# A decoder block on one core: the beginning of the attention in another order, the row sums a step later, and the gated branch's output products in halves

## The chip, the core and the metric

The kernel runs on one core of one Trainium2 chip. The time is the device time of one execution in microseconds (us); the figure for a kernel is the median of its runs. The profile is that of one execution, taken by the hardware profiler; its times count from the start of its span. PE is TensorE, DVE is VectorE, ACT is ScalarE, POOL is GpSimd and SP is SyncE, whose queue issues nearly all DMAs.

## The reference, cut to what matters

The block takes 1024 tokens of width 1024 in float32. From one projection of the normalised input come the queries, keys and values of eight heads of width 64, their forget gates, and the two inputs of a gated branch of width 512. The results of both are put side by side and go through one output matrix:

```python
c = jnp.cumsum(log_f, axis=1)
logits = einsum('bqhd,bkhd->bhqk', qi, k) * scale + ci[..., None] - c_k
p = softmax(where(causal, logits, -inf))
att = einsum('bhqk,bkhd->bqhd', p, v)
mixed = einsum('gij,bnjgd->bnigd', tril(w_s), rmsnorm(vg)) + b_s     # in chunks of 128 tokens
sg = u * mixed
h = x + concatenate([att, sg]) @ w_out
h = h + conv_ffn(rmsnorm(h))                                        # gated, causal convolution of width 3
out = rmsnorm(h)
```

So `att` meets rows 0 to 511 of `w_out` and `sg` rows 512 to 1023; the two partial products can be made at different times and added.

## The kernel before

Every float32 operand of a product is split in two parts, high and low (`[:, 0]` and `[:, 1]` of a tile), and a product is three matmuls: high by high, high by low, low by high. The splits are made by ACT (a copy, the cast) and DVE (a subtraction). The kernel has these parts in order of time: projections of the input (to about 214 us in the profile); the spatial products of the gated branch; the attention, head after head (to 387); the product of the attention's output with `w_out`; the second norm; the feed-forward part, 22 column blocks and then the down projection.

**Order.** A scheduling pass puts the instructions of each engine in an order, by the program's order and by when it reckons their operands to be ready, and each engine then runs its own in that order. `after(tc, later, earlier)` (line 60) forces an order of two instructions of one engine. `seq` (673) does so for every PE instruction of the attention, so that PE runs those in exactly the program's order. The class `Line` (30) wraps ACT, DVE and POOL: while it is `on`, each call stands behind the one before; while it is off and its `last` is set, each call stands behind that one instruction.

**Banks.** PSUM has eight banks, held by pools: `psa` for the projections and the spatial products (tags `b` and `s`, four banks each), `psb` from line 762 on for the attention (tag `b`, four banks, and tag `L`, two tiles of two banks for the logits), `psc` for what follows. A pool gives its banks to tags in the order in which the tags are first used. A tile of the next pool waits for what used its bank in the pool before.

**End of the projections** (710 to 720). The last products of the values fill four `s` banks. `spatial` (679) computes `mixed`: for each of eight groups three matmuls into a `b` bank and two DVE operations that add the bias and multiply by `u` in place in `ut`. `evac_v` (655) empties a bank of values into `V`, with ACT for the high part and DVE for the low. A small exponential (719) is there to have ACT's table of that function loaded.

**Beginning of the attention** (912 to 920). `head_loads(h)` (766) issues five DMAs for a head: queries `qd`, keys `kd` three times (512 KB, 256 KB, 256 KB), and a broadcast of the summed gates `ncd` (512 KB); the queries are 512 KB too, so a head is 2 MB. `turn_sg(hf)` (698) transposes half of the gated branch's result: four banks with four 128x128 transposes each, and the two parts of the split from each bank. `logits(h, j)` (778) takes query block j of head h: matmuls over the keys 0 to (j+1)*128 into an `L` tile, a mask on POOL (790), a DVE operation that adds the gates and keeps the least value `mn` (798), and ACT's exponential, which also adds up the row (800). The mask of block j changes columns that the DVE operation of block j+1 reads, so it waits for that one. Head 0's eight blocks come first of all, from j = 7 down.

**Attention steps** (921 to 943). A head has five steps. In each, `turn_p` (802) transposes two pairs of key blocks of the probabilities for the next step (a bank each, copied by ACT and subtracted by DVE into `pt`, 814 and 815); `values` (818) multiplies the present ones with `V` into the bank `po`, which ACT and DVE empty twice a head (840, 841); and one or two blocks of the next head's logits follow each. At step 1 `row_tail` (733) inverts the head's eight row sums (738), transposes them (739), sends them to memory and loads them back in another layout (741, 742); `pair_half` (745) multiplies by them, for heads 0 to 5 on POOL, for the last pair on DVE (756 to 758).

**Fillers.** `sg_out` (845) is a generator with the gated branch's products with `w_out`. It loads the weights of one half of the columns (`wos`, two DMAs of 512 KB), splits them (`split`, ACT and POOL), and then makes 16 products, each of 128 tokens by 512 columns: twelve matmuls over four blocks of the contraction into one bank, an addition of `x` on DVE (877), a store to `hpd` (878). `fill(key)` (908) takes the next product, as often as the table `FILLS` (21) says for that place: once after j = 5, 3 and 0 of head 0's logits (key (-1, j)), and in heads 0 to 4 after steps 0, 2, 4 (even heads) or 1, 3 (odd heads). Heads 5 to 7 have none.

**After the attention.** `wmm` (1022) makes the product with the other rows of `w_out`, of which the loop at 1086 does three quarters of the contraction for eight banks before the last heads' part is needed.

Of the kernel before, what the change touches and what calls it, by code (L numbers as in the profile page):

```python
# [65 lines left out]
def block_kernel(ctx: ExitStack, tc: tile.TileContext, xT, xtok, wuv, wv, wqk, wf, cpk, bfv,  # L66
# [37 lines left out]
    def f32(ap):  # L104
        return ap.bitcast(F32)
# [549 lines left out]
    def evac_v(tt, ps):  # L655
        if tt % 2 == 0:
            V.append(sb("V", [P, 2, 8, 2, 64], F32R))
        v = V[tt // 2]
        p3 = ps.rearrange("p (h d) -> p h d", h=8)
        act.activation(v[:, tt % 2, :, 0, :], p3, AF.Copy, scale=rstd1[:, tt:tt + 1])  # L660
        dve.scalar_tensor_tensor(out=v[:, tt % 2, :, 1, :], in0=p3, scalar=rstd1[:, tt:tt + 1],
                                 in1=f32(v[:, tt % 2, :, 0, :]), op0=ALU.mult, op1=ALU.subtract)

    for p_ in range(2):
        t = ring(F32)
# [32 lines left out]
    def turn_sg(hf):  # L698

        for c in range(4):  # L700
            if hf == 0:
                sgT[c] = sb("G", [P, 2, 1024], F32R)
            ps = bank()
            for t in range(4):
                seq(pe.transpose(ps[:, t * P:(t + 1) * P], ut[hf][:, t, c * P:(c + 1) * P], ident))
            o = slice(hf * 512, hf * 512 + 512)
            act.copy(sgT[c][:, 0, o], ps)
            dve.tensor_tensor(out=sgT[c][:, 1, o], in0=ps, in1=f32(sgT[c][:, 0, o]), op=ALU.subtract)

    S = [sbank() for _ in range(4)]  # L710
    for k in range(4):
        tmul(S, w0[k], "T3", k, True)
        pool.tensor_tensor(out=wvr[k][:, 1, :], in0=wvr[k][:, 0, :], in1=wvr[k][:, 1, :], op=ALU.add)
    tprod(S, lambda k: wvr[k][:, 1, :], "B22", False)
    spatial()
    for m in range(4):
        evac_v(4 + m, S[m])

    act.activation(pad[:, 0:1], eps, AF.Exp)
    act.last = dve.last = None  # L720


# [53 lines left out]
        rows[h] = sml.tile([P, 8], F32, tag="rs", name=nm("rs"))  # L776

    def logits(h, j):


        i, jj, hh = j // 2, j % 2, h % 2
        A, B, ck, B2 = abs_[h][:, 0, :], abs_[h][:, 1, :], cks[:, hh, :], b2s[:, hh, :]
# [10 lines left out]
        ps = psa.tile([P, 1024], F32, tag="L", bufs=2, name=nm("pl"))  # L793
        for c in range(0, n, 512):
            e = min(n, c + 512)
            seq(pe.matmul(ps[:, c:e], A[:, qs], B[:, c:e], start=True, stop=False))  # L796
            seq(pe.matmul(ps[:, c:e], A[:, qs], B2[:, c:e], start=False, stop=True))  # L797
        dve.tensor_tensor_reduce(out=t, in0=ps[:, 0:n], in1=ck[:, 0:n], scale=1.0, scalar=lim[:, 0:1],  # L798
                                 op0=ALU.add, op1=ALU.min, accum_out=mn)
        exs.append(act.activation(t, t, AF.Exp, bias=mn, scale=-1.0, accum_out=rows[h][:, j:j + 1]))  # L800

    def turn_p(g):
# [42 lines left out]
    def sg_out():  # L845
# [14 lines left out]
            return whs  # L860

        whs = split(load(0), "pool")
        for hf in range(2):
            o = slice(hf * 512, hf * 512 + 512)
            for tt in range(8):
                if hf == 0 and tt == 6:
                    nxt = load(1)
                ts_ = slice(tt * P, (tt + 1) * P)
                hs = sb("raw", [P, 512])
                sp.dma_start(out=hs, in_=xtok[ts_, o])  # L870
                ps = fbank()
                for k in range(4):
                    w = whs[k]
                    seq(pe.matmul(ps, sgT[k][:, 0, ts_], w[:, 0, :], start=(k == 0), stop=False))  # L874
                    seq(pe.matmul(ps, sgT[k][:, 0, ts_], w[:, 1, :], start=False, stop=False))  # L875
                    seq(pe.matmul(ps, sgT[k][:, 1, ts_], w[:, 0, :], start=False, stop=(k == 3)))  # L876
                dve.tensor_tensor(out=hs, in0=ps, in1=hs, op=ALU.add)
# [32 lines left out]
            next(filler, None)  # L910

    head_loads(0)
    head_loads(1)
    turn_sg(0)
    for j in range(7, -1, -1):
        logits(0, j)
        if j == 6:
            turn_sg(1)
        fill((-1, j))
    turned = [turn_p(g) for g in STEPS[0]]  # L920
    for n, step in enumerate(STEPS):
# [3 lines left out]
        if h == 7 and s == 0:  # L925
# [590 lines left out]
```

## Time and profile before

| | us |
|---|---|
| median of 3 runs | 1076.2 (1076.04 to 1078.09) |
| the profiled execution | 1076.44 |
| its span | 1074.7 |
| PE busy | 1054.8 (98%) |
| PE weight loads busy (beside PE) | 875.8 (81%) |
| DVE busy | 892.9 (83%) |
| ACT busy | 571.0 (53%) |
| POOL busy | 237.2 (22%) |

How to read its rows. In a timeline a row has start, duration, engine, line of the code, operation, output tile <- input tiles, shape, and how many instructions were put together; in brackets stands how long the engine was idle before, and what it waited for. A row of the view of waits has waiter <- what it waited for: total us, times, longest. A row of the chain of waits has start, duration and what that stretch was spent on. Where `Line` makes the call the line is that of the helper, L44, and tiles tell the operations apart. A matmul's row is longer (0.39 us for 512 columns) than its distance to the next one in a row of matmuls, since they overlap.

### The profile page before, as it was taken

How to read it: one execution, taken by the hardware profiler on the slowest of the kernel's cores; microseconds unless marked ns; L12 is line 12 of the kernel's file. 1: busy time of each engine (PE TensorE's matmuls, PEld its weight loads, DVE VectorE, ACT ScalarE, POOL GpSimd, SP SyncE). 2: the span in 40 equal slices, each digit the busy share in tenths (PEclk: the TensorE clock that was granted, in tenths of full speed). 3: DMA queues.
4: the chain of work that ended last, by engine and by line, in shares of the span. 5: the costliest groups of instructions: out<-in, count | busy, mean ns of one | idle time of the engine just before them, and what ended most of it. 6: DMA issues, size and time to landing. Idle time of an engine off the chain costs nothing.

```text
span 1074.7 us, 14461 instructions
## 1 busy us (share of the span) xinstructions
PE 1054.8 (98%) x5013; PEld 875.8 (81%) x5013; DVE 892.9 (83%) x1303; ACT 571.0 (53%) x985; POOL 237.2 (22%) x219
## 2 busy tenths in 40 slices
PE   9999999989999899999999999999999999999997
PEld 6888788778888788878888888888888888888886
DVE  5985798777777869999899999989988776898774
ACT  6666644456666845764444444444444444454653
POOL 0002134020223651054333333333322000000000
PEclk9999999999999999999999999999999999999999
DMA  9242257957556335132244523223331899433442
GB/s 338 97 140 97 68 159 213 265 165 215 162 177 225 120 128 185 72 118 97 98 137 161 172 69 127 99 98 99 107 118 46 289 327 319 123 95 97 140 125 96
DMA packets 66297, 160.80 MB, mean 150 GB/s; under 512 B 7976, under 2 KB 8240, under 8 KB 66224
## 3 DMA queue, kind: packets, MB, share of 16 engines
q1 hardware_dynamic: 65792, 159.32, 45.5%
q8 instruction: 39, 0.64, 0.2%
q10 hardware_dynamic: 432, 0.57, 0.1%
q14 instruction: 34, 0.28, 0.1%
HBM read 117.06 MB, written 42.80 MB: 149 GB/s over the span
## 4 chain that ended last, share of the span: by engine, by line
PE 74%; DVE 2%; issue 2%; DMA 2%; ACT 2%; POOL 0%; DVEq 0%; ACTq 0%; POOLq 0%; SPq 0%
PE k L1369 19%; PE qa L1117 11%; PE qc L1117 11%; PE qd L1117 11%; PE qb L1117 5%; PE pb L832 2%; PE pb L813 2%; PE pf L874 1%; PE pf L876 1%; PE pf L875 1%; PE pl L796 1%; PE pl L797 1%; DMA raw<-wos 1%; PE pb L1026 1%; PE pb L1028 1%
## 5 line engine op out<-in xcount | busy, mean ns | idle before, releaser
L1369 PE MATMUL k<-whb,wha 128*128 128x512 f32 x924 | 209.7, 389 | 0.0
L1369 PEld LDWEIGHTS k<-whb,wha 128*128 128x128 f32 x924 | 173.3, 188 | 36.2 <-DVE wha L160 0.2
L1117 PE MATMUL qc<-xT,whb 128*128 128x512 f32 x540 | 129.8, 389 | 0.0
L1117 PE MATMUL qa<-xB,wha 128*128 128x512 f32 x528 | 127.2, 390 | 0.0
L1117 PEld LDWEIGHTS qc<-xT,whb 128*128 128x128 f32 x540 | 101.3, 188 | 21.2 <-ACT whb L154 0.2
L1117 PEld LDWEIGHTS qa<-xB,wha 128*128 128x128 f32 x528 | 98.8, 188 | 20.8 <-DVE wha L160 0.4
L154 ACT CAST wha<-sg 128x512 fp32r<-128x512 f32 x77 | 47.7, 622 | 96.9 <-PE k L1369 86.6
L154 ACT CAST whb<-sg 128x512 fp32r<-128x512 f32 x82 | 50.6, 618 | 85.8 <-PE qc L1117 68.5
L160 DVE TENSOR_TENSOR wha<-sg,wha 128x512 fp32r<-128x512 f32 x77 | 52.8, 688 | 41.0 <-ACT wha L154 40.9
L1117 PE MATMUL qd<-xB,whb 128*128 128x512 f32 x264 | 63.8, 389 | 0.5 <-DVE h L1236 0.5
L1117 PE MATMUL qd<-xT,whb 128*128 128x512 f32 x264 | 63.6, 389 | 0.0
L815 DVE TENSOR_TENSOR pt<-pb,pt 128x512 fp32r<-128x512 f32 (+1 forms) x80 | 50.0, 635 | 14.5 <-ACT pt L814 13.4
L160 DVE TENSOR_TENSOR whb<-sg,whb 128x512 fp32r<-128x512 f32 x82 | 58.3, 711 | 4.4 <-ACT whb L154 4.3
L1117 PE MATMUL qb<-xT,whb 128*128 128x512 f32 x252 | 60.8, 389 | 0.0
L1004 POOL TENSOR_TENSOR sg<-raw 128x512 f32<-128x512 f32 x20 | 30.9, 1546 | 134.2 <-DVE whb L160 76.0
L1117 PEld LDWEIGHTS qd<-xB,whb 128*128 128x128 f32 x264 | 49.5, 188 | 11.2 <-issue 0.9
L1117 PEld LDWEIGHTS qd<-xT,whb 128*128 128x128 f32 x264 | 49.5, 188 | 10.3
L1117 PEld LDWEIGHTS qb<-xT,whb 128*128 128x128 f32 x252 | 47.3, 188 | 9.8
L814 ACT CAST pt<-pb 128x512 fp32r<-128x512 f32 (+1 forms) x80 | 42.5, 539 | 20.6 <-PE pb L813 14.7
L832 PE MATMUL pb<-pt,V 128*128 128x256 f32 x320 | 51.4, 285 | 1.3 <-DVE pt L815 1.2
L790 POOL TENSOR_SCALAR_AFFINE_SELECT x<-x 128x128 f32<-128x128 f32 x64 | 19.9, 312 | 129.7 <-DVE mn L798 77.4
L1007 POOL TENSOR_TENSOR sg<-sg,raw 128x512 f32<-128x512 f32 x20 | 33.3, 1664 | 64.1 <-DVE whb L160 64.1
(396 smaller groups left out, 2305.7 us busy)
## 6 DMA issues: line engine op xcount, KB each, us to landing
raw<-wup SPq DMA_DIRECT2D x44, 512.0 KB, 3.7
sg<-hx SPq DMA_DIRECT2D x77, 256.0 KB, 2.6
hx<-hs SPq DMA_DIRECT2D x44, 256.0 KB, 3.8
hx<-ca SPq DMA_DIRECT2D x35, 256.0 KB, 2.0
xT<-wdn SPq DMA_DIRECT2D x28, 256.0 KB, 4.3
raw<-wqk SPq DMA_DIRECT2D x8, 512.0 KB, 3.6
qd<-G SPq DMA_DIRECT2D x16, 256.0 KB, 3.5
kd<-G SPq DMA_DIRECT2D x16, 256.0 KB, 3.3
```

The source lines that it names most:

```text
L154: act.copy(h, src)
L160: return eng.tensor_tensor(out=l, in0=src, in1=f32(h), op=ALU.subtract)
L790: sels[h].append(pool.affine_select(out=ck[:, qs], in_=ck[:, qs], pattern=[[-1, P]], compare_op=ALU.is_ge, fill=BIG, base=0, channel_multi ...
L796: seq(pe.matmul(ps[:, c:e], A[:, qs], B[:, c:e], start=True, stop=False))
L813: seq(pe.transpose(ptr[:, c:c + P], tj[jj][:, k * P:(k + 1) * P], ident))
L814: act.copy(pt[:, 0, 0:w], ptr[:, 0:w])
L815: dve.tensor_tensor(out=pt[:, 1, 0:w], in0=ptr[:, 0:w], in1=f32(pt[:, 0, 0:w]), op=ALU.subtract)
L832: seq(pe.matmul(po[0][:, oo:oo + n], lhs, pt[:, s, o:o + n], start=(k == 0 and s == 0), stop=(s == 1 and half)))
L1004: pool.tensor_tensor(out=s[0], in0=a21, in1=a22, op=ALU.add)
L1007: pool.tensor_tensor(out=s[3], in0=s[1], in1=a12, op=ALU.add)
L1117: pe.matmul(ps, w[:, wi, ks], xb[:, xi, k, :], start=(first and n == 0), stop=(n == 11), skip_group_check=True)
L1369: pe.matmul(banks[bk + m], xh[:, xi, ms], wh[:, wi, :], start=(first and p_ == 0 and n == 0), stop=(p_ == NP - 1 and n == 2), skip_group_c ...
```

## The change

Six edits, which belong together:

1. The four evictions of values come before `spatial` in the program, and the small exponential is ordered behind the last of them on ACT.
2. `sg_out` stops once after its first load and split, and this first part runs right after `head_loads(0)`, ahead of `head_loads(1)`; its ACT instructions are ordered behind the last eviction of values.
3. `logits` is cut in two, `logits_mm` (the matmuls) and `logits_end` (mask, minimum, exponential). Head 0's matmuls for j = 7 and 6 come ahead of `turn_sg(0)`, their ends behind its last DVE operation; then comes `turn_sg(1)`, then the fillers and the other blocks.
4. A filler is cut in two halves of the contraction, each with a bank, six matmuls and a DVE addition of its own; the store follows the second. The split of the second weights goes in two parts behind the halves of the eighth product.
5. `FILLS` counts halves: two after j = 6, 4 and 2 and one after j = 0 of head 0, and one in each of the 25 steps of heads 0 to 4. That makes 32 halves for the 16 products.
6. `row_tail` comes at step 2 of a head in place of step 1.

```diff
-FILLS = {(-1, j): 1 for j in (5, 3, 0)} | {(h, s): 1 for h in range(5) for s in ((0, 2, 4), (1, 3))[h % 2]}
+FILLS = {(-1, 6): 2, (-1, 4): 2, (-1, 2): 2, (-1, 0): 1} | {(h, s): 1 for h in range(5) for s in range(5)}
...
     tprod(S, lambda k: wvr[k][:, 1, :], "B22", False)
+    for m in range(4):
+        a = evac_v(4 + m, S[m])
+
+    after(tc, act.activation(pad[:, 0:1], eps, AF.Exp), a)
     spatial()
-    for m in range(4):
-        evac_v(4 + m, S[m])
-
-    act.activation(pad[:, 0:1], eps, AF.Exp)
     act.last = dve.last = None
...
+    def logits_mm(h, j):
+        A, B, B2 = abs_[h][:, 0, :], abs_[h][:, 1, :], b2s[:, h % 2, :]
+        n = (j + 1) * P
+        qs = slice(j * P, (j + 1) * P)
+        ps = psa.tile([P, 1024], F32, tag="L", bufs=2, name=nm("pl"))
+        for c in range(0, n, 512):
+            e = min(n, c + 512)
+            seq(pe.matmul(ps[:, c:e], A[:, qs], B[:, c:e], start=True, stop=False))
+            seq(pe.matmul(ps[:, c:e], A[:, qs], B2[:, c:e], start=False, stop=True))
+        return ps
+
+    def logits_end(h, j, ps, behind_=None):
...
+        if behind_ is not None:
+            after(tc, m, behind_)
...
         whs = split(load(0), "pool")
+        yield
...
-                ps = fbank()
-                for k in range(4):
-                    w = whs[k]
-                    seq(pe.matmul(ps, sgT[k][:, 0, ts_], w[:, 0, :], start=(k == 0), stop=False))
-                    seq(pe.matmul(ps, sgT[k][:, 0, ts_], w[:, 1, :], start=False, stop=False))
-                    seq(pe.matmul(ps, sgT[k][:, 1, ts_], w[:, 0, :], start=False, stop=(k == 3)))
-                dve.tensor_tensor(out=hs, in0=ps, in1=hs, op=ALU.add)
-                sp.dma_start(out=hpd[tt, :, o], in_=hs)
-                if hf == 0 and tt == 7:
-                    whs = split(nxt, "dve")
-                yield
+                for kh in range(2):
+                    ps = fbank()
+                    for k in (2 * kh, 2 * kh + 1):
+                        w = whs[k]
+                        seq(pe.matmul(ps, sgT[k][:, 0, ts_], w[:, 0, :], start=(k % 2 == 0), stop=False))
+                        seq(pe.matmul(ps, sgT[k][:, 0, ts_], w[:, 1, :], start=False, stop=False))
+                        seq(pe.matmul(ps, sgT[k][:, 1, ts_], w[:, 0, :], start=False, stop=(k % 2 == 1)))
+                    dve.tensor_tensor(out=hs, in0=ps, in1=hs, op=ALU.add)
+                    if kh == 1:
+                        sp.dma_start(out=hpd[tt, :, o], in_=hs)
+                    if hf == 0 and tt == 7:
+                        whs[2 * kh:2 * kh + 2] = split(nxt[2 * kh:2 * kh + 2], "dve")
+                    yield
...
     head_loads(0)
+    act.last = a
+    next(filler)
+    act.last = None
     head_loads(1)
-    turn_sg(0)
-    for j in range(7, -1, -1):
+    ahead_ = [(j, logits_mm(0, j)) for j in (7, 6)]
+    d = turn_sg(0)
+    for j, ps in ahead_:
+        logits_end(0, j, ps, d)
+    turn_sg(1)
+    fill((-1, 6))
+    for j in range(5, -1, -1):
         logits(0, j)
-        if j == 6:
-            turn_sg(1)
         fill((-1, j))
...
-        if s == 1:
+        if s == 2:
             if h % 2 == 0:
                 attF[h // 2] = sb("H", [P, 2, 1024])
             row_tail(h)
```

More of the change, by code (lines that the diff above doesn't have):

```diff
@@ L659, in evac_v @@
         p3 = ps.rearrange("p (h d) -> p h d", h=8)
[L660 removed]
+        a = act.activation(v[:, tt % 2, :, 0, :], p3, AF.Copy, scale=rstd1[:, tt:tt + 1])
         dve.scalar_tensor_tensor(out=v[:, tt % 2, :, 1, :], in0=p3, scalar=rstd1[:, tt:tt + 1],
                                  in1=f32(v[:, tt % 2, :, 0, :]), op0=ALU.mult, op1=ALU.subtract)
+        return a
     for p_ in range(2):
@@ L707, in turn_sg @@
             act.copy(sgT[c][:, 0, o], ps)
-            dve.tensor_tensor(out=sgT[c][:, 1, o], in0=ps, in1=f32(sgT[c][:, 0, o]), op=ALU.subtract)
+            d = dve.tensor_tensor(out=sgT[c][:, 1, o], in0=ps, in1=f32(sgT[c][:, 0, o]), op=ALU.subtract)
+        return d
     S = [sbank() for _ in range(4)]
@@ L778, in logits @@
     def logits(h, j):
+        logits_end(h, j, logits_mm(h, j))
+    def logits_mm(h, j):
[9 more added lines that the diff above has]
+    def logits_end(h, j, ps, behind_=None):
         i, jj, hh = j // 2, j % 2, h % 2
-        A, B, ck, B2 = abs_[h][:, 0, :], abs_[h][:, 1, :], cks[:, hh, :], b2s[:, hh, :]
+        ck = cks[:, hh, :]
         w1, w2 = (2 * i + 1) * P, (2 * i + 2) * P
@@ L792, in logits @@
         mn = sml.tile([P, 1], F32, tag="mn", name=nm("mn"))
[L793 to L799, printed above, removed]
+        m = dve.tensor_tensor_reduce(out=t, in0=ps[:, 0:n], in1=ck[:, 0:n], scale=1.0, scalar=lim[:, 0:1],
+                                     op0=ALU.add, op1=ALU.min, accum_out=mn)
+        if behind_ is not None:
+            after(tc, m, behind_)
         exs.append(act.activation(t, t, AF.Exp, bias=mn, scale=-1.0, accum_out=rows[h][:, j:j + 1]))
```

## The prediction

> **What bounds the kernel now.** I read the page first, then the busy times of three windows, then what TensorE (PE) waited for, then the timelines of PE, VectorE (DVE) and ScalarE (ACT) at those waits. "Step" below is one of the five attention steps of a head.
>
> ```profile
> span 1074.7 us, 14461 instructions
> PE 1054.8 (98%) x5013; PEld 875.8 (81%) x5013; DVE 892.9 (83%) x1303; ACT 571.0 (53%) x985; POOL 237.2 (22%) x219
> ```
>
> PE is busy for 98% of the span, so the change can win only where PE waits. It touches three stretches: from the end of the spatial products to the first transposes of probabilities; heads 0 to 4, which have fillers; heads 5 to 7, which have none. The windows view gives one row for each (its length, then the busy us and instructions of PE, weight loads, DVE, ACT and POOL, the granted clock, and the DMA's share and GB/s):
>
> ```profile
> 219.60:239.55 19.95, 16.84 (x93) 14.07 (x92) 15.11 (x33) 14.28 (x29) 7.06 (x11) 1.00 0.36 128
> 239.55:346.40 106.85, 104.77 (x670) 91.99 (x669) 80.42 (x164) 69.51 (x151) 25.04 (x53) 1.00 0.64 195
> 346.40:387.10 40.70, 35.66 (x274) 32.83 (x272) 33.21 (x69) 31.96 (x70) 24.36 (x36) 1.00 0.37 121
> ```
>
> PE is idle for 3.11, 2.08 and 5.04 us: 10.2 us is all that could be won if every gap in the three closed. DVE is the next busiest: 80.42 of 106.85 us where the fillers are. The view of waits says whom PE waited for between 219 and 400 us (us in total, times, longest):
>
> ```profile
> PE pb L813 <- DVE pt L815: 2.9, 6, 0.7
> PE pb L739 <- DVE rs L738: 2.6, 2, 1.5
> PE pb L705 <- DVE V L44: 1.9, 1, 1.9
> PE pb L832 <- DVE pt L815: 1.2, 3, 0.6
> PE pl L796 <- DVE mn L798: 1.2, 2, 0.7
> ```
>
> Every wait is for DVE: for a bank that it has yet to empty (L813, L705, L796), or for its result. L739 is the row sums' transposition; the change moves it.
>
> **Part 1, the beginning of the attention.** Its rows, DVE, ACT and PE:
>
> ```profile
> 213.06 2.11 DVE L44 SCALAR_TENSOR_TENSOR V<-ps,rstd,V 128x512 fp32r<-128x512 f32 x3 [2.84 <-ACT V L44]
> 215.09 6.35 DVE L44 SCALAR_TENSOR_TENSOR A<-pb,cp,A 128x256 f32<-128x256 f32 x16
> 221.35 0.74 DVE L44 SCALAR_TENSOR_TENSOR V<-ps,rstd,V 128x512 fp32r<-128x512 f32 x1
> 223.86 2.48 DVE L708 TENSOR_TENSOR G<-pb,G 128x512 fp32r<-128x512 f32 x4 [1.77 <-ACT G L707]
> 212.33 2.73 ACT L44 ACTIVATE V<-ps,rstd 128x512 fp32r<-128x512 f32 x4 [4.81 <-PE ps L258]
> 220.94 2.40 ACT L154 CAST whl<-raw 128x512 fp32r<-128x512 f32 x4 [5.88 <-DMA raw<-wos]
> 226.98 1.28 ACT L800 ACT_TABLE_LOAD   x1
> 222.15 1.53 PE L705 MATMUL pb<-ident,A 128*128 128x128 f32 x12 [1.93 <-DVE V L44]
> 225.25 1.91 PE L705 MATMUL pb<-ident,A 128*128 128x128 f32 x16
> 239.55 1.80 PE L813 MATMUL pb<-ident,t 128*128 128x128 f32 x15
> ```
>
> Before, one V eviction stood behind the sixteen gating operations, and the transposes of the gated branch waited for its bank until 222.15. With the four V evictions first, DVE does them from 213.06 to 215.8 (4 x 0.70) and the gating to 222.15 (+6.35). DVE's work is only reordered: it ends as late as before. What is won is what PE does meanwhile: the logits of j = 7 and 6 (1.8 us before: from the end of the twelve transposes, 0.11 us each after 222.15, to 225.25) go into the 1.93 us gap, if head 0's operands are there; by the chain they had landed at 210.42:
>
> ```profile
> 203.47 6.95 DMA x<-kd
> 210.50 11.69 DMA raw<-wos
> ```
>
> A pool gives its banks out in the order of first use: before, the transposes came first and got the banks of V (hence their wait for V). Now the logits come first and get those, and the transposes get the banks of the spatial products, the last of which DVE frees at 222.15. If the first transposes fall on that one, PE waits for 0.9 us at 221.3; if on the first freed one, not at all. I take the wait, since before the second transposes fell on the bank emptied last.
>
> From 222.15 on: 16 transposes take 1.9 us (to 224.1); DVE subtracts at 0.6 us each and ends the first half at about 225.7 (226.34 before). It then has the minima of j = 7 and 6 (1.27 and 1.14 us), and only then the second half's subtractions, except one that fits where the minimum of j = 6 waits for its mask. All four banks are held by the second half, so the first half filler starts at about 227.6 and the second at 229.25: PE idles for 1.7 us here, a new wait. After that PE has six half fillers and the logits of j = 5 to 0. A whole filler is twelve matmuls:
>
> ```profile
> 232.27 0.39 PE L874 MATMUL pf<-whl,G 128*128 128x512 f32 x1
> 234.99 0.33 PE L796 MATMUL pl<-x 128*128 128x384 f32 x1
> ```
>
> From its first matmul to what follows it 2.72 us pass, so a half is 1.36. Six halves are 8.2 us and the logits 2.5, which makes 240.0; with the kind bank order 239.0. I take 239.6, against 239.55: **0.0 us**, between -0.9 and +0.8, with 3.5 fillers done in place of 3. Three things hang on covers. The weights' load (1 MB) is issued ahead of head 1's five loads. By the second of those rows it took 11.69 us before with head 1's 2 MB and 0.25 MB of head 0 ahead of it, 0.28 MB per us; behind head 0 alone it lands about 4.6 us after 210.4, at 215, so its four casts (2.40 us) stand on ACT before 222, where the copies of the transposes begin; if it landed at 222 as before, the copies and all behind them would be 1.7 us later. Head 1's loads come 3.6 us later; they landed before 222, and their logits begin only after the transposes at 239.55. The exponential's table load (1.28 us) goes to 215, where ACT is idle; before it delayed no exponential that PE waited for. What the new loads queue behind on SP is head 0's, which have to land first anyway.
>
> **Part 2, half a filler in each step.** Heads 0 to 4 hold 25 halves for 13 whole fillers: **-1.36 us** of PE, which part 1 has taken over. Of the 2.08 us that PE is idle in these heads, five waits for `pt` make 1.67 (a first one of 0.20 for its values, four of transposes for a bank, of 0.26 to 0.7; the first and the last of these):
>
> ```profile
> 258.24 0.63 PE L813 MATMUL pb<-ident,H 128*128 128x128 f32 x4 [0.26 <-DVE pt L815]
> ...
> 341.91 0.63 PE L813 MATMUL pb<-ident,H 128*128 128x128 f32 x4 [0.26 <-DVE pt L815]
> ```
>
> The four stand at the end of a head, where transposes follow a step that had no filler: DVE had not emptied the bank. With 1.36 us of filler in every step they should go. But each half has an addition of its own, so that there are 32 for 16. DVE's timeline has one and its neighbour:
>
> ```profile
> 280.67 0.68 DVE L877 TENSOR_TENSOR raw<-pf,raw 128x512 f32<-128x512 f32 x1
> 281.27 1.28 DVE L160 TENSOR_TENSOR whl<-raw,whl 128x512 fp32r<-128x512 f32 x2
> ```
>
> An addition holds DVE for 0.60 us from start to start. Twelve more are 7.2 us in heads 0 to 4: DVE goes to 87.6 of some 105 us. On average it is covered by PE; in the last two steps of a head it is not by much (an estimate by the columns of their products and DVE's operations gives 7.0 us of PE and 6.8 of DVE). What is queued behind an addition there are the subtractions of `pt`, for which `values` and the next transposes wait. So I count only half of the 1.67 as won, **-0.8 us**; the ends are -1.7 (all) and +6.0 (an addition on the path in the last two steps of all five heads, 10 x 0.60).
>
> The Trainium skill, VectorE: DVE Perf Modes, "The DRAIN you can't avoid", says that after each operation the pipe has to empty for about the operation's duration less 266 ns before the next starts. By that an addition would take about 1.1 us (estimate) and the twelve 13 us, not 7.2. With that the sum below would come to about +2.4 in place of -3.4. The two rows just above start 0.60 us apart, so the trace contradicts it here; as a mechanism it is the last of the rivals.
>
> **Part 3, row sums a step later.** PE's two waits of 2.6 us, and what stood around them:
>
> ```profile
> 364.21 1.27 DVE L798 CUSTOM_DVE_ANT_0 H<-pl,x,lim 128x1024 f32<-128x1024 f32 x1
> 365.41 0.20 DVE L738 RECIPROCAL rs<-rs 128x8 f32<-128x8 f32 x1
> 365.75 0.27 PE L739 MATMUL pb<-ident,rs 128*8 128x128 f32 x1 [1.51 <-DVE rs L738]
> 380.07 1.28 ACT L946 ACT_TABLE_LOAD   x1
> 380.67 0.27 PE L739 MATMUL pb<-ident,rs 128*8 128x128 f32 x1 [1.11 <-DVE rs L738]
> ```
>
> One step later the sums are long ready, and PE goes on with the next transposes (0.9 us), values and logits. What is late next is the banks of these transposes: their copies on ACT, then their subtractions on DVE. In head 6 DVE is in the long minimum until 365.41, so that the two subtractions end at 366.6, about when PE would be back for the banks (364.1 + 2.6 us of a step); DVE is busy for 33.21 of the 40.70 us, so I count 0.9 of the 1.51. In head 7 ACT loads a table until 381.4, and the copies come after it as they do now: 0.3 of the 1.11. Together **-1.2 us**, between 0 and -2.6. Heads 0 to 5 show no such wait.
>
> **The sum**: 0.0 - 1.36 - 0.8 - 1.2 = -3.4 us. The profiled execution took 1076.44 us (span 1074.7 and 1.7 around it; 0.2 above the median of the three runs). 1076.44 - 3.4 = 1073.0. After 387 the feed-forward part is PE's alone, so that a shift there reaches the end.
>
> **The rivals.** A difference under 0.2% (2.15 us) is about what a measurement cannot tell from none: faster is below 1074.0, slower above 1078.4.
>
> *DVE pushes back* (0.22): the twelve additions cost as many waits as they remove and 2 us more, and part 3 gives half: 0 - 1.36 + 2.0 - 0.6 = 0.0, 1076.5, no change. For it speaks DVE's 6.8 of 7.0 us at the end of each head; against it 26 us of DVE that are free in heads 0 to 4.
>
> *The last bank* (0.10), slower. The view of PE, DVE and the queues around the end of the attention:
>
> ```profile
> 381.74 0.27 ACTq L741 DMA_DIRECT2D rsd<-t  x1
> 385.44 0.45 SPq L742 DMA_DIRECT2D H<-rsd  x1
> 389.23 0.39 PE L1026 MATMUL ps<-whl,A 128*128 128x512 f32 x1
> 391.69 0.69 DVE L756 TENSOR_TENSOR H<-H 128x512 f32<-128x512 f32 x1 [4.21 <-DMA H<-rsd]
> 392.41 0.69 DVE L841 TENSOR_TENSOR H<-pb,H 64x512 f32<-64x512 f32 x1
> ```
>
> DVE empties the last bank of `values` (L841) only behind a product that waits for the row sums' way through memory. With the logits' banks now first, the output product's second group (389.23) takes one of the four banks that `values` and the transposes share. If it is that last one, PE waits for L841; and head 7's row sums now leave a step of some 1.8 us later, so that L841, which ended at 393.1, ends 5.7 us after PE gets there (394.9 less 389.2, both earlier by what was won). Price +5.7: 1078.7. It decides only if one bank of four is hit and L841 stays behind L756.
>
> *All waits go* (0.17): the bank order is kind (-0.9), the 1.67 and the 2.6 us go: -0.9 - 1.36 - 1.7 - 2.6 = -6.6, 1069.9. For it speaks that each wait has a cover; against it the busy DVE and ACT behind two of them.
>
> *The change doesn't do what it says* (0.04): the weights land as late as before, and the copies wait for them: +1.7 on the forecast, 1074.7. *An addition costs DVE double* (0.02): if DVE were held past the 0.60 us of the rows for as long again, an addition would cost 1.2 us, the two of a head's last steps 1.2 more than counted, and DVE's 6.8 would be 8.0 against 7.0 of PE: five heads by 1.0, with none of the 0.8, 0 - 1.36 + 5 - 1.2 = +2.4, 1078.9. This is about what the page named in part 2 would give; the row of 0.60 speaks against it. The forecast has 0.45.
>
> **The numbers.** Predicted 1073.0 us. The forecast's own bounds are 1070.8 to 1075.5. The range of 8 in 10 takes in most of the rivals on both sides: 1069.3 to 1077.5. Faster: most of 0.45 and all of 0.17, 0.58; within 0.2%: 0.30; slower 0.12.
>
> **What would show it.** Right: no PE wait for V at 220; logits of j = 7 and 6 ahead of the first transposes; casts of the weights before 219; a PE idle of 1 to 2 us ahead of the first half filler; no wait for `rs`; PE idle of under 1.5 us in heads 0 to 4; 32 additions of 0.69 us. Wrong: DVE over 90% in heads 0 to 4 with PE waiting for `pt`; PE waiting for DVE in the first groups of the output product; the copies of the transposes behind the weights.

## The result: 0.34% slower

| | before | after |
|---|---|---|
| median, us | 1076.3 (1075.68 to 1078.09) | 1079.98 (1078.56 to 1081.65) |
| ratio of the times, 95% interval | | 1.0034 (1.0021 to 1.0047) |
| the profiled execution, us | 1076.44 | 1079.75 |

The forecast was 1073.0, the range 1069.3 to 1077.5: wrong in sign. Each ratio, here and below, is taken against the kernel before as it ran in the same round (medians from 1076.3 to 1077.05), so it can differ a little from the quotient of two medians shown.

The page of the kernel after:

```profile
span 1078.0 us, 14473 instructions
PE 1056.9 (98%) x5013; PEld 875.4 (81%) x5013; DVE 899.8 (83%) x1319; ACT 569.1 (53%) x985; POOL 237.6 (22%) x219
```

The sixteen more additions are there (DVE has 1319 instructions for 1303 and 6.9 us more), and PE has the same 5013 matmuls. The windows view of the kernel after (columns as in the prediction), cut at the first transposes of probabilities, behind the last filler and at the output product:

```profile
219.60:240.49 20.89, 19.18 (x101) 15.16 (x100) 17.22 (x36) 10.69 (x22) 4.88 (x11) 1.00 0.28 89
240.49:348.07 107.58, 103.78 (x665) 90.50 (x663) 86.66 (x176) 67.29 (x151) 24.72 (x53) 1.00 0.61 192
348.07:389.05 40.98, 36.10 (x272) 33.13 (x271) 33.09 (x72) 32.35 (x74) 24.64 (x37) 1.00 0.43 125
```

The same cut of the kernel before (the prediction had cut 0.13 us earlier):

```profile
239.55:346.53 106.98, 104.90 (x671) 92.02 (x670) 80.48 (x164) 69.51 (x151) 25.04 (x53) 1.00 0.64 195
346.53:387.08 40.55, 35.51 (x272) 32.77 (x271) 33.13 (x68) 31.96 (x70) 24.36 (x36) 1.00 0.37 121
```

The start is 0.94 us longer with half a filler more in it, heads 0 to 4 are 0.60 us longer with half a filler (1.36 us) less, heads 5 to 7 are 0.43 us longer. With 0.98 us of a new wait in the output product and 0.35 us elsewhere that is the 3.3 us between the spans. Whom PE waits for in the kernel after, between 219 and 410 us (of the view of waits):

```profile
PE pb L826 <- ACT t L742: 1.9, 2, 1.5
PE pb L826 <- DVE raw L892: 1.8, 5, 0.4
PE pb L741 <- DVE rs L740: 1.6, 1, 1.6
PE pf L889 <- DVE G L709: 1.1, 1, 1.1
PE pb L845 <- DVE H L854: 1.0, 2, 0.6
PE ps L1048 <- DVE H L854: 1.0, 1, 1.0
PE pf L889 <- DVE pt L828: 0.8, 1, 0.8
PE pl L790 <- DVE mn L809: 0.7, 2, 0.4
PE pb L826 <- DVE pt L828: 0.7, 1, 0.7
```

In the changed file L826 is the transposes of probabilities, L741 the row sums', L845 `values`, L889 a filler's first matmul, L892 its addition. The old waits for `pt` and for V are mostly gone, as meant. New are five waits for a filler's addition, two for ACT's copy of the row sums (L742), three for the bank of `po` (two of `values`, one at the output product) and two of fillers for a bank (the one for `G`, ahead of the first half filler, was forecast). Four places in the timelines of PE:

```profile
250.80 0.66 PE L826 MATMUL pb<-ident,wy 128*128 128x128 f32 x4 [0.35 <-DVE raw L892]
370.05 0.27 PE L741 MATMUL pb<-ident,rs 128*8 128x128 f32 x1 [1.57 <-DVE rs L740]
384.61 0.55 PE L826 MATMUL pb<-ident,H 128*128 128x128 f32 x3 [1.46 <-ACT t L742]
396.39 0.50 PE L1048 MATMUL ps<-whl,A 128*128 128x512 f32 x1 [0.98 <-DVE H L854]
```

and DVE and ACT at them:

```profile
250.05 0.69 DVE L892 TENSOR_TENSOR raw<-pf,raw 128x512 f32<-128x512 f32 x1 [0.23 <-PE pf L891]
...
368.64 1.14 DVE L809 CUSTOM_DVE_ANT_0 H<-pl,x,lim 128x896 f32<-128x896 f32 x1
...
369.71 0.20 DVE L740 RECIPROCAL rs<-rs 128x8 f32<-128x8 f32 x1
...
394.93 0.69 DVE L758 TENSOR_TENSOR H<-H 128x512 f32<-128x512 f32 x1 [5.48 <-DMA H<-rsd]
395.65 0.69 DVE L854 TENSOR_TENSOR H<-pb,H 64x512 f32<-64x512 f32 x1
```

```profile
381.96 1.28 ACT L968 ACT_TABLE_LOAD   x1
...
383.36 1.06 ACT L827 CAST pt<-pb 128x512 fp32r<-128x512 f32 x2
384.31 0.25 ACT L742 COPY t<-pb 8x128 f32<-8x128 f32 x1
```

At 250.05 DVE was idle and waiting for the filler: the addition begins as soon as it can, and PE still waits for the bank that it frees. That is no busy DVE, it is a bank too few. At 369.71 the reciprocal has moved along with the transposition and is late again, behind a minimum; at 384.31 the copy stands behind the table load and two casts that the load held up; at 395.65 the last eviction stands behind L758, which waits for the row sums' way through memory.

### The profile page after: what moved, and what is told of

Same layout as the page of the kernel before. It is cut to its first block, busy times and chain, and to the rows that moved or that the text cites. A ratio compares the mean times of both kernels' runs of the same rounds, so it can differ in the third digit from the quotient of the medians.

```text
span 1078.0 us, 14473 instructions
## 1 busy us (share of the span) xinstructions
PE 1056.9 (98%) x5013; PEld 875.4 (81%) x5013; DVE 899.8 (83%) x1319; ACT 569.1 (53%) x985; POOL 237.6 (22%) x219
## 4 chain that ended last, share of the span: by engine, by line
PE 68%; DVE 3%; ACT 1%; issue 1%; POOL 1%; DMA 1%; SPq 0%; DVEq 0%; ACTq 0%
PE k L1391 19%; PE qa L1139 11%; PE qc L1139 11%; PE qd L1139 11%; PE qb L1139 5%; PE pb L845 2%; PE pb L826 1%; PE pb L1048 1%; PE pb L1049 1%; PE pb L1050 1%; PE pl L790 1%; PE pl L791 1%; PE ps L1084 1%; PE pf L889 1%; DMA H<-rsd 1%
## 5 line engine op out<-in xcount | busy, mean ns | idle before, releaser
L845 PE MATMUL pb<-pt,V 128*128 128x256 f32 x320 | 51.6, 286 | 1.2 <-DVE H L854 1.0
```

The source lines that it names most:

```text
L845: seq(pe.matmul(po[0][:, oo:oo + n], lhs, pt[:, s, o:o + n], start=(k == 0 and s == 0), stop=(s == 1 and half)))
```

## The experiments

Theory A: the change costs banks. In a step `po` holds one of the four shared banks, the two transposes two, the half filler the fourth; the row sums' transposition, or a second `po` at a head's turn, is one too many. Theory B, the prediction's rival: the additions cost, by DVE's time. Theory C: the row sums' new place costs. "Heads 0-4" is the length of that stretch in the profile, cut as above (106.98 before, 107.58 after).

| kernel | median, us | ratio to before (95%) | heads 0-4 |
|---|---|---|---|
| e1_sums_at_1 | 1081.67 | 1.0052 (1.0038 to 1.0065) | 109.40 |
| e2_sums_only | 1077.23 | 1.0008 (0.9999 to 1.0017) | 106.80 |
| e3_start_only | 1076.29 | 0.9999 (0.9990 to 1.0008) | 107.27 |
| e4_halves_only | 1089.33 | 1.0119 (1.0105 to 1.0133) | 109.40 |
| e5_extra_adds | 1089.82 | 1.0120 (1.0107 to 1.0133) | 111.39 |
| e6_columns | 1079.65 | 1.0026 (1.0016 to 1.0036) | 107.02 |
| e7_filler_in_logits_bank | 1089.05 | 1.0114 (1.0101 to 1.0127) | 113.35 |
| e8_last_bank | 1079.65 | 1.0033 (1.0020 to 1.0045) | 107.61 |
| e9_evict_first | 1079.31 | 1.0024 (1.0015 to 1.0033) | 107.59 |
| e10_rowsum_bank | 1077.25 | 1.0001 (0.9992 to 1.0010) | 104.39 |
| e11_before_sums | 1073.97 | 0.9978 (0.9966 to 0.9990) | 106.82 |
| e12_after_all | 1073.64 | 0.9963 (0.9951 to 0.9976) | 104.41 |
| e13_last_store | 1079.18 | 1.0023 (1.0012 to 1.0033) | 107.60 |
| e14_all_store | 1071.04 | 0.9947 (0.9935 to 0.9960) | 104.42 |
| e15_whole_fillers | 1073.28 | 0.9968 (0.9955 to 0.9980) | 106.61 |
| e16_before_repaired | 1074.01 | 0.9971 (0.9960 to 0.9983) | 106.29 |
| e17_mask_order | 1070.83 | 0.9943 (0.9931 to 0.9955) | 104.39 |
| e18_mask_alone | 1078.74 | 1.0020 (1.0011 to 1.0028) | 107.61 |

**The parts alone.** e1 is the changed kernel with the row sums back in the second step:

```diff
-        if s == 2:
+        if s == 1:
```

> The changed kernel (1080.0 us) with one thing undone: the row sums go back from the third to the second step of each head. Theory A, banks: with a half filler in every step, the step that also turns the row sums asks for one bank of four more than come free, and the transposes behind it wait 0.35 to 0.4 us in each of heads 0 to 4; the later sums also hold the last bank of the values 1 us longer at the first groups of the output product. In the second step head by head the shortage is the same, so only part of the 2 us goes, but the 1.0 us at the output product goes: about 1078.5. Theory B, additions: the sixteen more additions hold DVE, whatever the banks: 1079 to 1080, only the 1.0 us may go. Theory C, the row sums' new place is what costs: 1076 to 1077.

e2 is the kernel before with the opposite edit:

> The kernel before (1076.3 us) with the row sums one step later and nothing else. Theory A: no bank is short in a step without a filler, and a whole filler stands in the third step of heads 0, 2 and 4 only: at most 3 x 0.4 us of new waits against 0.5 to 1.5 us that heads 6 and 7 win: 1075.5 to 1076.5. Theory C: 1078 or more, with a wait of about 1 us at the first groups of the output product and waits for the row sums' bank in the third steps.

e3 has the changed beginning alone:

```diff
+FILLS = {(-1, j): 1 for j in (6, 4, 2)} | {(h, s): 1 for h in range(5) for s in ((0, 2, 4), (1, 3))[h % 2]}
```

> The changed beginning alone: order of V, of the weights' load, the early logits and the turning of the gated branch, but whole fillers as before (three of them ahead of the first transposes of probabilities, then one in every second step) and the row sums in their old place. All theories: the beginning ended 0.94 us later in the changed kernel with half a filler (1.36 us) more done, so alone it wins 0.4 us: 1075.9; it loses instead (1077 or more) if the order of the banks that it changes also costs at the end of the attention, where the output product's second group then waits for the last bank of the values.

e4 has the halves alone, in the kernel before:

```diff
+FILLS = {(-1, 5): 2, (-1, 3): 2, (-1, 0): 3} | {(h, s): 1 for h in range(5) for s in range(5)}
```

> The kernel before with halves of fillers alone: seven ahead of the first transposes of probabilities (1.36 us later there), one in each of the 25 steps of heads 0 to 4 (1.36 us less there), row sums and beginning as before. Theory A: the waits come from banks that a half filler in every step takes away, those of the row sums' step above all: 1077.5 to 1078.5, with new waits of the transposes for an addition in the second step of each head. Theory B: the sixteen more additions of 0.6 us push DVE in all steps, so the loss of heads 0 to 4 is there whole, 2 us and spread: 1078.4. Theory C: no loss without the move of the row sums: 1076 to 1076.5.

C falls: undoing the move makes the changed kernel slower still (1.0052), and the move alone costs at most 0.17%. A's figures fail too: e1 was to be 1078.5 and is 1081.67 (the 0.98 us at the output product did go), e2 was to be 1076.5 at most and is 1077.23. The beginning alone cannot be told from nothing (0.9990 to 1.0008, that is 1.1 us faster to 0.9 slower). All the loss comes with the halves, and in e4 far more of it (13 us) than any theory said. Heads 0 to 4 take 109.40 us in both kernels with halves and the row sums in the second step, 2.4 us over the kernel before with half a filler less, and 1.8 us over the changed kernel, which has as many tenants one step later: the place counts too, and the mere number of banks does not explain that. Of the rest of e4's loss 0.8 us lie ahead of these heads, 1.8 in heads 5 to 7 (not explained here), and most at the output product; its PE and DVE there, and the windows of the wait and of what follows it:

```profile
397.14 0.77 PE L1028 MATMUL pb<-whl,A 128*128 128x512 f32 x1 [5.04 <-DVE H L841]
```

```profile
395.59 0.69 DVE L756 TENSOR_TENSOR H<-H 128x512 f32<-128x512 f32 x1 [3.26 <-DMA H<-rsd]
396.31 0.68 DVE L841 TENSOR_TENSOR H<-pb,H 64x512 f32<-64x512 f32 x1
```

```profile
392.10:397.10 5.00, 0.00 (x1) 0.00 (x0) 1.68 (x4) 1.20 (x2) 0.00 (x0) 0.86 0.89 290
397.10:402.40 5.30, 5.26 (x12) 4.13 (x13) 4.62 (x6) 2.70 (x5) 1.94 (x2) 0.50 0.52 209
```

By the bank addresses of the compiled programs the last `po` has here the bank that the first group of the output product takes; in the changed kernel it is the fourth group's, in the kernel before the fifth's. This is the prediction's rival "the last bank", and its price has a second part: 5.04 us of waiting, and then 5.3 us at a granted clock of 0.50, another 2.6 us (half of 5.3).

**Additions or banks.** e5 is the kernel before with twelve operations of an addition's size on DVE that change no number:

```diff
+        if 0 <= key[0] < 5 and key not in FILL:
+            hs = held[0][1]
+            after(tc, dve.tensor_tensor(out=hs, in0=hs, in1=hs, op=ALU.max), order[0])
+            store()
```

> The kernel before with whole fillers, and in each of the twelve steps of heads 0 to 4 that have no filler one more operation on DVE, of the size of an addition (128x512, a maximum of the filler's sum with itself, which changes no number), placed behind the step's products; no bank of TensorE is taken by it. The two last evictions of the values stand ahead of the pair's products, so that the bank that happens to be last costs nothing. Theory B, additions: the 12 x 0.60 us push DVE, and the 5 us that halves alone lost before the output product come back here: 1079.5 to 1081.5. Theory A, banks: an operation that holds no bank is covered: 1076 to 1077.

Its median would speak for B, and misleads. From head 2's row sums to head 5's, the kernel before and e5:

```profile
288.56:349.18 60.62, 59.84 (x389) 52.94 (x388) 45.15 (x94) 39.03 (x87) 17.76 (x34) 1.00 0.64 201
```

```profile
292.36:352.86 60.50, 59.76 (x387) 52.97 (x388) 48.41 (x101) 39.32 (x87) 19.96 (x36) 1.00 0.64 187
```

Seven more operations on DVE (94 to 101) and not a tenth of a us longer. Nearly all that e5 lost it lost at two places of its own making: a load of `x` that came late (issued at 271.44 us; the edit puts a store ahead of each such load in SP's queue), and the last bank, 6.54 us, since the order of evictions that it was to have did not come about (the scheduling pass had put L756 between them again). The first, on PE and DVE:

```profile
276.17 0.90 PE L813 MATMUL pb<-ident,gg 128*128 128x128 f32 x3 [2.33 <-DVE raw L879]
```

```profile
275.42 0.69 DVE L879 TENSOR_TENSOR raw<-pf,raw 128x512 f32<-128x512 f32 x1 [3.57 <-DMA raw<-xtok]
```

So B falls for these seven operations. e6 has the halves by columns:

```diff
+                    ps = fbank()[:, 0:256]
+                    n = slice(kh * 256, kh * 256 + 256)
...
+                    dve.tensor_tensor(out=hs[:, n], in0=ps, in1=hs[:, n], op=ALU.add)
```

> The changed kernel with the fillers halved by their columns (twelve products of 256 columns) and not by their contraction: as much of PE in each step, as many banks taken, but each addition half as long, so that the additions' sum on DVE is about as before the change. Theory A: the bank is still taken last in a step and asked for again in the next; only the addition that frees it is 0.3 us shorter: waits for the filler's addition go from 0.4 to about 0.1, 1078 to 1079. Theory B: DVE has its 6 to 7 us back and the new waits go: 1075 to 1076.5.

Heads 0 to 4 fall to 107.02 and four of the five waits for an addition go, as A said; the median is 0.7 us above A's 1078 to 1079 (B's 1075 to 1076.5 is further off). e7 moves the half fillers to the logits' banks:

```diff
-        return psa.tile([P, 512], F32, tag=FTAG, bufs=FB, name=nm("pf"))
+        return psa.tile([P, 1024], F32, tag="L", bufs=2, name=nm("pf"))[:, 0:512]
```

> The changed kernel with the half fillers in the logits' banks (two of 128x1024) and not in the four that transposes and values share. Theory A: the waits of transposes and values for an addition, and the row sums' step's shortage, go; the logits may wait for a minimum or an addition more in the first steps: 1076.5 to 1078. Theory B: the additions stay on DVE, so the time stays: 1079 to 1081.

Both expectations fail. PE's first waits there:

```profile
PE pf L889 <- DVE mn L809: 6.2, 10, 2.2
```

No transposition waits for an addition any more, but the filler now waits for a minimum to empty its bank, and the logits for the filler: the shortage is moved to a place with less slack. e10 takes away another tenant, the smallest:

```diff
-        ptr = bank()
+        ptr = psa.tile([P, 1024], F32, tag="L", bufs=2, name=nm("pr"))
```

> The changed kernel with the row sums' transposition in one of the two logits' banks and not in one of the four shared ones: one tenant less in the third step of each head, the same work everywhere. Theory A, banks: the five waits of 0.35 to 0.41 us of the second transposes for a half filler's addition go, unless the logits now wait for their bank: 1078.2. Theory B, additions: no change, 1080.

The windows view of its heads 0 to 4:

```profile
240.00:344.39 104.39, 103.15 (x664) 90.61 (x663) 86.66 (x176) 67.41 (x151) 24.92 (x53) 1.00 0.64 198
```

3.2 us less than in the changed kernel, with the same 86.66 us of DVE and the same 176 operations on it. The five waits (1.8) are gone, and so are the one of a filler for `pt` (0.8) and one of two of `values` for `po` (0.4); a new one of 0.3 us has come. That is 2.7 of the 3.2 us; the rest stands in no row of the waits. The median falls by 2.7 us, the intervals of the two ratios lie apart, and this although heads 5 to 7 took 2.3 us longer in its profile, by a wait that is found below. The stretch repeats to 0.03 us in all four kernels with this edit and halves by the contraction (104.39 to 104.42) and in all five without it that have the changed halves and row sums (107.58 to 107.61). A is shown here: with a half filler in every step, one tenant of one bank costs 3.2 us. With whole fillers the same move gains 0.5 (106.29 in e16 for 106.82 in e11).

**The end of the attention.** e8 puts the pair products of head 7 behind both evictions in the program:

```diff
-            if h == 7:
+            if h == 7 and i == 0:
+                pair_half(3, slice(512, 1024))
                 pair_half(3, o)
```

> The changed kernel with the pair's products for head 7 (which wait for the row sums' way through memory) put behind both evictions of the values. Theory of the last bank: the 0.98 us that the output product's fourth group waits go and nothing else changes, 1079.0; a rival: the products move with it and what is behind them is late instead, no change, 1080.

The scheduling pass put the instructions back in the old order, so this tests nothing. The wait was absent in its profile only because the row sums landed 1.2 us earlier. e9 has the order written out:

```diff
+            after(tc, dve.tensor_tensor(out=f[:, 0, o], in0=f[:, 0, o], in1=f[:, 1, o], op=ALU.mult), lastd[0])
```

> The changed kernel with both evictions of the values, by an order written out, ahead of head 7's pair products on DVE (in the try before, DVE's order had stayed as it was). Theory of the last bank: the wait of 0.98 us at the output product goes in every execution, 1079.0, and the executions lie closer together if it is the landing of the row sums through memory that spreads them (1078.6 to 1081.7 in the changed kernel). Rival: that wait only took the place of another one, 1080.

The ratio falls by 0.0010, about the 0.98 us, but the intervals overlap; what is shown is that the wait is gone from the profile. The spread of its executions (1078.0 to 1082.3) is no smaller, so it does not come from there. e11 moves the row sums, but not the reciprocal, and the table load too, with e9's order of evictions:

```diff
+        if s == 1:
+            dve.reciprocal(rows[h], rows[h])
+        if s == 2:
...
-    after(tc, act.activation(pad[:, 0:1], eps, AF.Sqrt), exs[-1])
+    after(tc, act.activation(pad[:, 0:1], eps, AF.Sqrt), lastc[0])
```

> The kernel before (1076.5) with part 3 done without its two companions: the reciprocal of the row sums stays in the second step, only the transposition and what follows goes to the third; the table load behind the attention's last exponential goes behind ACT's last copy of the values; both evictions ahead of the pair's products. With the move alone, 1.6 us of waiting for the reciprocal (head 6), 1.5 for ACT behind the table load (head 7) and 0.4 at the output product remained. Theory, placement: these three go, 1073.5 to 1074.5. Rival, handed on: the transposes of the probabilities wait for their banks in place of them, 1076 or more.

The two waits that the move alone had kept are gone and 2.4 us are won (0.22%), where the move alone won nothing; the third, 0.4 us at the output product, is still there. The two waits of e2 that this removed:

```profile
PE pb L739 <- DVE rs L738: 1.6, 1, 1.6
...
PE pb L813 <- ACT t L740: 1.5, 1, 1.5
```

**All repairs, and what halves are worth.** e12 is the changed kernel with the edits of e9, e10 and e11:

> The changed kernel with all four: evictions first, row sums in a logits' bank, reciprocal in the second step, table load behind the last copy. By the waits that its profile shows, 1.0 + 1.8 + 1.6 + 1.5 us go: 1074. Rival, handed on: half of them come back as waits of transposes and values for a bank, 1077. If the halves cost more than the sum of visible waits, it stays slower than the kernel before with the same repairs.

It lands at the expected 1074, but with one new large wait. Its PE, DVE and POOL:

```profile
356.86 0.87 PE L827 MATMUL pb<-ident,gg 128*128 128x128 f32 x3 [3.05 <-DVE pt L829]
```

```profile
355.22 1.02 DVE L810 CUSTOM_DVE_ANT_0 t<-pl,x,lim 128x768 f32<-128x768 f32 x1 [3.42 <-POOL x L807]
```

```profile
354.64 0.55 POOL L807 TENSOR_SCALAR_AFFINE_SELECT x<-x 128x128 f32<-128x128 f32 x2 [3.97 <-DMA x<-ncd]
```

Two masks in one row: head 7's first, which waits for head 7's gates, and behind it in POOL's queue head 6's, for which DVE and so PE wait. The changed kernel has the same at 356.05. On SP, the kernel after issues this load behind the store of the last filler, the kernel before ahead of it:

```profile
349.44 0.32 SPq L894 DMA_DIRECT2D hpd<-raw  x1
349.86 0.38 SPq L775 DMA_DIRECT2D x<-ncd  x1
```

```profile
345.72 0.32 SPq L773 DMA_DIRECT2D x<-ncd  x1
...
347.45 0.32 SPq L878 DMA_DIRECT2D hpd<-raw  x1
```

e13 moves that store alone, e14 in the repaired kernel:

```diff
+                for d, hs in held:
+                    after(tc, sp.dma_start(out=d, in_=hs), loads[7])
```

> The changed kernel with one thing moved: the store of the last filler's sum goes behind the loads of head 7 on SyncE, not ahead of head 7's column row (which the masks on GpSimd wait for). Theory, queue: the wait of 0.66 us at 358 us goes, and since it was 2.3 to 3.0 us in the profiles of kernels with the same queue, the median falls by 0.7 to 1.5: 1078.5 to 1079.3. Rival: the row lands no earlier, 1080.

> The changed kernel with the four repairs of before (evictions first, row sums in a logits' bank, reciprocal in the second step, late table load; 1073.6) and the last store behind head 7's loads. Theory, queue: the 3.05 us of its profile at 357 us go, 1070.6 to 1072. Rival: handed on to the next step, 1073.6.

Both medians fall where they were expected, e13's without being clear of the changed kernel's. But e14's wait is 1.60 us and not gone (0.31 for 0.66 in e13), so the queue of SP is half of it at most. That e14 still gains 2.6 us has a second part: in e12 the clock was low behind the wait, which costs about 1.5 us more (0.48 of 3.2), and in e14 it was not.

```profile
356.80:360.00 3.20, 3.14 (x13) 2.98 (x14) 2.75 (x6) 2.34 (x7) 1.93 (x3) 0.52 0.33 116
```

e17 and e18 order the masks:

```diff
+        if h == 7 and j == 7:
+            after(tc, sels[7][0], sels[6][-1])
```

> The changed kernel with all five repairs (1071.0) and head 7's first mask ordered behind head 6's last one on GpSimd. Theory, GpSimd's order: head 6's mask no longer stands behind one that waits for a load, and the 1.60 us at 354 us go: 1069.4. Rival: the load is as late for head 7's own logits and the wait comes back there, 1071.

> The changed kernel (1080.0) with only the order of the two masks changed. Theory, GpSimd's order: the wait of 0.66 us at 358 us in its profile goes, 1079.3, and since the wait was larger in other profiles with the same order (2.3 us), down to 1078.5. Rival, no part of the loss: 1080.

The place on PE in e14 and in e17:

```profile
354.72 0.52 PE L827 MATMUL pb<-ident,gg 128*128 128x128 f32 x3 [1.60 <-DVE pt L829]
```

```profile
354.26 0.52 PE L829 MATMUL pb<-ident,gg 128*128 128x128 f32 x3 [0.33 <-DVE pt L831]
```

With the masks in order the wait is 0.33 and 0.31 us, so it takes POOL's order for the late load to reach PE; how late the load is sets how long PE waits, and in e13 an earlier load alone gave 0.31 too. As time it is shown only weakly: e18's ratio is 0.0014 below the changed kernel's with overlapping intervals, and e17 wins 1.3 us of heads 5 to 7 in its profile but 0.2 in the median. e15 is e14 with whole fillers, e16 the kernel before with the five repairs:

> As the last one (all five repairs, the changed beginning), but with whole fillers: three ahead of the first transposes of probabilities, then one in every second step. If halves are worth what the prediction said (0.8 us of waits for a bank at the ends of heads) it is 0.8 to 1.7 us slower than the one with halves. If they bring nothing but twelve more beginnings and additions (0.6 us by the lengths of the blocks), it is 0 to 1 us faster. If banks are still short with halves, it is faster by more.

> The kernel before with the same five repairs: whole fillers and the old beginning. Differs from the last one in the beginning alone, which by the changed beginning alone (1076.3 against 1076.5) is worth nothing: within 0.7 us of it, 1071 to 1073.5. If the changed beginning gains once the end is repaired, it is slower by more than that.

No execution of e14 (1070.42 to 1071.76) is as slow as the fastest of e15 (1072.53): with the banks there, the halves win 2.2 us between the medians, 0.5 more than the most that was expected. The beginning (e15 against e16) cannot be told from nothing again; e16 came out 0.5 us above its expected 1071 to 1073.5. e17, the fastest, beats the kernel before by 0.57% (0.45 to 0.69).

## Why the prediction was wrong, point by point

Between the -3.4 us of the forecast and the +3.3 us between the two spans lie 6.7 us: 0.9 from part 1, 2.8 from part 2, 1.6 from part 3, 1.3 behind the attention. The largest is the step that decided.

**Part 1** (0.0, between -0.9 and +0.8; measured +0.94). The mechanism was right: V emptied by 215.8, gating to 222.0, the weights' casts from 216.4 to 218.6, the first half filler at 227.81 after an idle of 1.15 us (said: 227.6, 1.7). The working itself gave 240.0, and 239.6 was taken; the rest is a term that was mis-sized: the six half fillers and the logits behind the first half (1.36 us from 227.81) took 11.3 us to 240.49, not 10.7. And its 0.0 is a gain in disguise: with half a filler more done, which part 2 books as -1.36, the beginning itself was to win 1.36 us. In time it won nothing that e3, or e15 against e16, could show; in e3's profile the way from the first spatial product to the first transposes of probabilities is 0.73 us shorter (24.65 for 25.38).

**Part 2** (-2.16; measured +0.60) is the step that failed. The waits of which it said "With 1.36 us of filler in every step they should go" did go. What failed is the price that it set against them: the prediction counted PE's time and DVE's time for a half filler in every step, and put at nothing, without a reason, the bank that the half filler takes, the last of four. It looked for the cost in DVE (the rival "DVE pushes back"), where e5 finds none; DVE was busy for 81% of the stretch, not for the over 90% that was to be the sign, and the 0.60 us for an addition was right. The shortage alone is worth 3.2 us (e10). With the row sums' bank elsewhere the stretch falls by 2.57 us (104.41 in e12 for 106.98), within the part's own -1.36 and -1.67: the gain was there, and a shared bank took it away.

**Part 3** (-1.2, between 0 and -2.6; measured +0.43). "One step later the sums are long ready" failed: the reciprocal moved along and stood behind a minimum again (1.57 us in head 6), and the table load that had hidden in the old wait was now itself on the path (1.46 us in head 7, where the prediction had counted 0.3 us as won). And 0.66 us came by a queue that the prediction passed by: POOL's, behind a load that SP issues after the last half filler's store. With these taken away, heads 5 to 7 go from 40.55 to 36.39 us (e17), more than the part's whole bound.

**The last bank** (given 0.10) came true with another price: the fourth group and not the second, 0.98 us for 5.7; that its 1078.7 lies close to the measured time is chance, since most of the loss arose before. Its size depends on which bank the last `po` gets, which nothing in the change fixes: 0 to 6.5 us in these kernels, and more with the clock.

## What to carry to other kernels

When work is spread more evenly, count the tenants of a shared pool step by step, the small ones (a transposition of eight columns) too, before counting engine time. An operation that moves carries its companions: ask what its inputs' instructions stand behind in their new place, and which wait the old place had hidden. An experiment's median can be made by a place that the edit never meant (e4, e5): read the stretch that it was built for.

## What the runs showed of the hardware

A wait of PE of 2.3 us or more can cost more than itself. The granted clock was 0.50 for 5.3 us after 5.04 us of waiting (e4, above), 0.52 for 3.2 us after 3.05 us (e12, above), and in e5, after 2.33 us:

```profile
276.10:278.70 2.60, 2.53 (x9) 2.30 (x10) 2.41 (x6) 1.02 (x3) 0.69 (x1) 0.50 0.00 0
```

In e9 a wait of 2.27 us was followed by the full clock:

```profile
PE pb L828 <- DVE pt L830: 2.3, 1, 2.3
```

```profile
359.70:362.00 2.30, 2.23 (x17) 2.14 (x18) 2.30 (x6) 2.15 (x6) 1.94 (x3) 1.00 0.52 135
```

The Trainium skill, TensorE: Matmul & The Clock Gate, "Part 1: The HAM clock gate", gives half the clock after an idle window of about 3.4 us that runs free; half the clock agrees with these rows, a wait of 2.33 us being enough does not follow from its 3.4. Whether it is the length of the wait or the moment at which it falls that parts 2.33 from 2.27 us, these two waits cannot tell.

The table load took 1.28 us; it began when the instruction ahead of it had ended, and the next one began 1.29 us after it had. The Trainium skill, ScalarE: Activation LUTs, "What ACT_TABLE_LOAD costs", adds 1.38 us for emptying the pipe to that; the trace disagrees, no such time stands in these rows:

```profile
381.74 0.20 ACT L813 ACTIVATION_READ_ACCUMULATOR gg<-gg,mn 128x1 f32 x1
381.96 1.28 ACT L968 ACT_TABLE_LOAD   x1
383.25 0.20 ACT L968 ACTIVATE pad<-eps 128x1 f32<-128x1 f32 x1
```
